# A hybrid encoder block on one core: the recurrence's preparations earlier among the input blocks, its chunks spread over six blocks, gate products inside the chunks

## The chip, the cores and the metric

The kernel runs on one core of a Trainium2 chip. The metric is the device time of one execution in microseconds (us); the median of three runs of the kernel before is 879.84 us (878.81 to 880.39). The engines are TensorE (PE: matmuls, with its weight loads as PEld), VectorE (DVE), ScalarE (ACT), GpSimd (POOL) and SyncE (SP, which issues most DMAs). Every engine works through its own instructions strictly in its own order.

## What is computed

One layer of a streaming encoder, for 512 positions of width 1024. The part that matters here is the first third: an input projection, a recurrence over 8 heads of 64 (branch a), a gated linear recurrence of width 512 behind a convolution over four positions (branch b), and their merge. Cross-attention and a convolutional feed-forward network (FFN) follow and are not touched.

```python
h = rms_norm(x, norm_mix_g[l])
proj = h @ w_in[l] + b_in[l]          # 38 blocks of 128 columns
y_a = rwkv7_branch(proj[..., :cb0], ...) @ w_branch_a[l]
y_b = rglru_branch(proj[..., cb0:cb1], proj[..., cb1:cb2], ...) @ w_branch_b[l]
merged = sigmoid(proj[..., cb2:cg1]) * y_a + sigmoid(proj[..., cg1:]) * y_b
x = x + merged @ w_mix_out[l]
...
# rwkv7_recurrence, per head and position
sa = state @ a_t
state = state * w_t + sa * b_t + v_t * k_t
y_t = state @ r_t
...
# rglru_branch
xb = causal_dwconv(px, conv_w, conv_b)
gate_a, gate_x = sigmoid(xb * w_ga + b_ga), sigmoid(xb * w_gx + b_gx)
h_t = a_t * h_(t-1) + xb_t * gate_x_t * mult_t
y = h * gelu(py)
```

## The kernel before

**Input blocks.** `inproj(i)` (L645) makes block i of the projection, the PSUM tile `in_ps{i}`, with 48 matmuls of 256 columns. A float32 weight is split in two fp32r halves, `win_h` (cast on ACT, L176) and `win_l` (the rest, on DVE, L177), and the product is made of three terms. The halves have three buffers each in the pool `wp` (L118), the raw weights four, so the casts of one block's weights can only begin when PE has finished the block three places earlier. Weights are streamed in the order IN_ORDER: blocks 12, 13, 4, 5, 0, 1, 8, 9, 6, 7, 2, 3, 10, 11 (those of the recurrence), then 22 to 37 (the merge's gates), 14 to 17 (branch b's convolution input) and 18 to 21 (its gelu gate). PSUM has three buffers for these tiles (`mm_ps`, L129), so a block starts only when the block three earlier has been read out.

**Preparations.** For each head pair j = 0 to 3, blocks 4+j (k), j (r) and 8+j (v) are read out with the shift over positions (`evac_shift`, L651). `prep(j)` (L673) makes the decay and rate (PE tiles psw, psa; a scan `L` and exponentials); `prep2(j)` (L691) normalizes k (PE tile ss) and writes the operands AK and KBt on DVE; `scores(j)` (L739) makes 32 small products within the 8 chunks of 64 positions (PE tiles sc), which are masked back into AK and BZ and sent to DRAM as dM; `bonus_terms(j)` (L716) makes the bonus, which is read back and multiplied later (`bonus`, L721, PE tiles bo). The loop over `jp` (L769) works on two pairs at a time, and NEARLY = 3 gate blocks (22 to 24) stand ahead of the last preparation.

**Inverse.** Once dM is complete, it is loaded as Nm, and 31 steps on DVE (L820 and L821: `zz`, `Zt`) invert the 32x32 diagonal blocks. The result goes to DRAM and comes back as ZA and as a part of BZ (L837, L842); PE completes the 64x64 inverses with zh0, zo0, zh16, zo16.

**Chunks.** `chunk(c)` (L911), for c = 0 to 7 in turn, is a chain through PE, ACT and DVE: x (PE), a copy Xs (DVE), u (PE), copies into UV (ACT and DVE), s (PE), Sn and the next UV (DVE), and x of the next chunk. vr and kbr put rows into chunk form, y is the output. PSUM has one buffer each for the tags kv, xu, y and s.

**Branch b.** `px_gates(b)` (L1002) reads block 14+b into xb with one ACT and three DVE instructions (L1007) and a fix (L1009), multiplies it by two gate weights (PE tiles ga, gx) and makes the gates; `px_scan(b)` (L1022) finishes the gates and scans into YB (L1029). xb has two buffers, so xb2 takes the place of xb0 when px_scan(0) is done, and xb3 that of xb1. ga, gx and the group norm's gv0, gg0 share one PSUM buffer. `group_norm` (L973) normalizes half of branch a's output.

**The order on PE** is written out by hand: `ORDER` (L40) lists PE's tiles, `name:n` for the next n matmuls of a tile, a bare name for all that are left of it, and `PE.arrange` (L100, called behind the last product) ties each matmul to the one before it. The small float32 products stand between input blocks, so that PE has in_ps matmuls to do while the other engines work on the chain. DVE's and ACT's order is that of the program with priorities; casts of weights have a high one.

**Sums.** NSUM (L642) says how many sums of FFN weights POOL issues behind which input block.

Of the kernel before, what the change touches and what calls it, by code (L numbers as in the profile page):

```python
# [41 lines left out]
ORDER = """  # L42
in_ps4 in_ps5 in_ps0 in_ps1 in_ps8 in_ps9 psw0 psa0 ss0 in_ps6 in_ps7 in_ps2:6 sc0 in_ps2:12 psw1 psa1 in_ps2:18
ss1 in_ps2 in_ps3 in_ps10:30 sc1 in_ps10 in_ps11 psw2 psa2 ss2 in_ps22 in_ps23 in_ps24:6 sc2 in_ps24 psw3 psa3
ss3 in_ps25 in_ps26 in_ps27:30 sc3 in_ps27 in_ps28 bo0 in_ps29 bo1 in_ps30 bo2 in_ps31 bo3 in_ps32 in_ps33
in_ps34 in_ps35 in_ps36 in_ps37 in_ps14 in_ps15:42 ga0 in_ps15 in_ps16:2 gx0 in_ps16:38 ga1 in_ps16:6 zh0 gx1
in_ps16 in_ps17:4 zo0 zh16 in_ps17:10 zo16 in_ps17:10 vr0 in_ps17:6 x0 y0:8 kbr0 in_ps17:2 u0 vr1 in_ps17:6 s0
y0 kbr1 in_ps17:4 x1 y1:8 in_ps17:2 u1 vr2 in_ps17 s1 y1 kbr2 in_ps18:8 x2 y2:8 in_ps18:4 u2 vr3 s2 y2 kbr3 ga2
in_ps18:2 x3 y3:8 gx2 u3 vr4 s3 y3 kbr4 ga3 x4 y4:8 u4 vr5 gx3 s4 y4 kbr5 in_ps18:6 x5 y5:8 u5 vr6 in_ps18:6 s5
y5 kbr6 in_ps18:2 x6 y6:8 vr7 in_ps18:2 u6 in_ps18:10 s6 y6 kbr7 in_ps18 gv0_0:1 in_ps19:8 x7 y7:8 in_ps19:6 u7  # L50
in_ps19:6 gv0_0 y7 in_ps19:4 gg0_0 in_ps19:20 gv0_1 in_ps19 in_ps20:16 gg0_1 in_ps20 in_ps21 gv1_0 gg1_0 gg1_1
yb_ps0:18 yb_ps1:10 gv1_1 yb_ps1:8 yb_ps0 yb_ps1 yb_ps2 yb_ps3 yb_ps4 yb_ps5 yb_ps6 yb_ps7 ya_ps0 ya_ps1 ya_ps2
ya_ps3 ya_ps4 ya_ps5 ya_ps6 ya_ps7 mix_ps0 mix_ps1 mix_ps2 mix_ps3 mix_ps4 mix_ps5 mix_ps6 mix_ps7 q_ps0_0:32
rxc_ps q_ps0_0 q_ps0_1 q_ps1_0:24 sc_ps0_0 sc_ps0_1 q_ps1_0 q_ps1_1:4 sc_ps0_2 prT_ps0:2 q_ps1_1:8 sc_ps0_3
prT_ps0:2 q_ps1_1:18 prT_ps0 q_ps1_1:10 o_ps0 q_ps1_1 o_ps1 q_ps2_0:4 sc_ps1_0 sc_ps1_1 q_ps2_0:16 sc_ps1_2
prT_ps1:2 sc_ps1_3 prT_ps1:2 q_ps2_0:16 prT_ps1 q_ps2_0:10 o_ps2 q_ps2_0 q_ps2_1:18 o_ps3 q_ps2_1 q_ps3_0:16
sc_ps2_0 sc_ps2_1 q_ps3_0:14 sc_ps2_2 prT_ps2:2 sc_ps2_3 prT_ps2:2 q_ps3_0:16 prT_ps2 q_ps3_0 q_ps3_1:16 o_ps4
q_ps3_1:16 o_ps5 q_ps3_1 co_ps0:16 sc_ps3_0 sc_ps3_1 co_ps0:14 sc_ps3_2 prT_ps3:2 sc_ps3_3 prT_ps3:2 co_ps0:6
co_ps4:10 prT_ps3 co_ps4:10 o_ps6 co_ps4:12 o_ps7 co_ps4:4 co_ps0:6 co_ps4:6 co_ps0 co_ps4 co_ps1
""".split()  # L60


# [17 lines left out]
def hybrid_block_kernel(ctx: ExitStack, tc: tile.TileContext, xT_d, mT_d, pv_d, cst_d, win_d, wk_d, wv_d,  # L80
                        lup_d, gup_d, rga_d, rgx_d, wba_d, wbb_d, wmix_d, wq_d, wo_d, wfi_d, wfo_d, out_d):
    nc = tc.nc
    V, S = nc.vector, nc.scalar
# [76 lines left out]
    def stream(dram, name, between=None, order=None, at=0):  # L160

        for g in order or range(dram.shape[0]):
            with tc.high_priority():
# [9 lines left out]
                wdma.append(ins)
                hi, lo = weight_tiles(name, g, at)
                for o in range(0, 1024, n):
                    casts.append(S.copy(hi[:, o:o + n], raw[:, o:o + n]))  # L176
                    V.tensor_tensor(lo[:, o:o + n], raw[:, o:o + n], hi[:, o:o + n].bitcast(F32), ALU.subtract)  # L177
# [466 lines left out]

    def inproj(i):  # L645
        nonlocal last_in
        ps = mm_ps(f"in_ps{i}")
        last_in = dense(ps, uin, lambda kb: (h2[:, 0, kb, :], h2[:, 1, kb, :]), KB, NSUM.get(i, 0))
        return ps

    def evac_shift(ps, blk, out):  # L651
# [3 lines left out]
        V.scalar_tensor_tensor(out, ps, omu[:, blk:blk + 1], q, ALU.mult, ALU.add)  # L655
# [107 lines left out]
    def gate_block(b):  # L763
        ps = inproj(22 + b)
        sg = tp.tile([P, T], F32, tag="st", name=f"gs{b}", bufs=2)
        tab(sg, ps, AF.Sigmoid, bias=par("b_in", 22 + b))
        nc.scalar.dma_start(dG[b], sg)

    for jp in range(2):  # L769
        js = (2 * jp, 2 * jp + 1)  # L770
        pks, prs = {}, {}
        for j in js:
            pks[j] = pp.tile([P, T], F32, tag="pk", name=f"pk{j}", bufs=2)
            evac_shift(inproj(4 + j), 4 + j, pks[j])
        for j in js:
            prs[j] = pp.tile([P, T], F32, tag="pr", name=f"pr{j}", bufs=3)
            evac_shift(inproj(j), j, prs[j])
        for j in js:
            evac_shift(inproj(8 + j), 8 + j, vT[:, j, :])
        for j in js:  # L780
            if j == 3:
                for i in IN_REST[:NEARLY]:
                    gate_block(i - 22)
            at, L, Pp = prep(j)
            prep2(j, pks[j], prs[j], at, L, Pp)
            scores(j)
            bonus_terms(j, pks[j], prs[j])
# [19 lines left out]
    with tc.tile_pool(name="pz", bufs=1, reuse_waits="tile") as pz:
        Nm = pz.tile([P, 32, 32], F32, name="Nm")
        Zt = pz.tile([P, 32, 32], F32, name="Zt")
        Zn = pz.tile([P, 32, 32], F32, name="Zn")  # L810
# [5 lines left out]
        V.memset(Zt.rearrange("p a b -> p (a b)")[:, 0:1024:33], 1.0)  # L816
        for s in range(30, -1, -1):
            n = 31 - s
            t3 = zz[:, 0:n * n].rearrange("p (a b) -> p a b", b=n)
            V.tensor_tensor(t3, Zt[:, s + 1:, s + 1:], Nm[:, s:s + 1, s + 1:].to_broadcast([P, n, n]), ALU.mult)  # L820
            V.tensor_reduce(Zt[:, s + 1:, s:s + 1], t3, AX.X, ALU.add)  # L821
# [804 lines left out]
```

## Time and profile before

| | |
|---|---|
| median of three runs | 879.84 us |
| profiled execution | 879.42 us, span 877.6 us |
| PE busy | 855.6 us, 97% |
| DVE busy | 679.5 us, 77% |
| ACT busy | 514.0 us, 59% |
| POOL busy | 132.5 us, 15% |
| granted TensorE clock | 0.998 |

A row of a timeline gives the start and the duration in us, the engine, the line, the operation, the tiles (out<-in), how many instructions, and in brackets the idle time before them with what ended it. A row of a window gives its length, and then for each engine its busy time and in (x...) its instructions; PEclk, the share of the DMA engines and GB/s stand at its end. A row of groups gives total busy us, mean ns of one, and the idle time before them.

### The profile page before, as it was taken

What the parts mean: (1) busy time and instruction counts of PE and PEld (TensorE: products, weight loads), DVE (VectorE), ACT (ScalarE), POOL (GpSimd) and SP (SyncE); (2) the same over time, 40 slices, a digit from 0 to 9 for tenths busy, and PEclk for the clock granted to TensorE, in tenths of its full rate; (3) what the DMA queues carried; (4) which work ended last, traced back from release to release, by engine and by line L of the source; (5) the groups of instructions that cost most, each with busy time, mean ns of one, the idle gap of its engine ahead of it and who ended that gap; (6) DMA issues with size and microseconds to landing.
All of it is one profiled execution on the core that took longest, in us unless ns stands there. A gap on an engine that the chain in (4) does not pass through costs nothing.

```text
span 877.6 us, 19313 instructions
## 1 busy us (share of the span) xinstructions
PE 855.6 (97%) x7884; PEld 825.9 (94%) x7884; DVE 679.5 (77%) x1096; ACT 514.0 (59%) x788; POOL 132.5 (15%) x163
## 2 busy tenths in 40 slices
PE   9999989999999999999999999999999999999996
PEld 8889989999997789999999899999999999999996
DVE  6796598877967686685575568799888888999774
ACT  7575676743437687234454356666666566867563
POOL 0102223021101022001122211102111121111100
PEclk9999999999999999999999999999999999999999
DMA  8888799777895479858987858999999999998953
...
DMA packets 97576, 201.60 MB, mean 230 GB/s; under 512 B 19600, under 2 KB 30992, under 8 KB 97424
## 3 DMA queue, kind: packets, MB, share of 16 engines
...
q8 instruction: 62, 1.02, 0.5%
...
## 4 chain that ended last, share of the span: by engine, by line
PE 74%; DVE 13%; ACT 5%; DMA 4%; issue 3%; DVEq 0%; ACTq 0%; SPq 0%
PE fx_ps L95 14%; PE in_ps L95 13%; PE fyz_ps L95 10%; PE ox_ps L95 7%; PE oyz_ps L95 5%; PE co_ps L95 5%; PE mix_ps L95 4%; PE q_ps L95 4%; PE yb_ps L95 2%; DVE win_l L177 2%; PE v_ps L95 2%; PE o_ps L95 1%; PE k_ps L95 1%; DVE Zt L821 1%; DVE zz L820 1%
## 5 line engine op out<-in xcount | busy, mean ns | idle before, releaser
L95 PE MATMUL in_ps<-hT,win_h 128*128 128x256 f32 x1216 | 214.8, 280 | 2.1 <-DVE pr L655 1.6
L95 PEld LDWEIGHTS in_ps<-hT,win_h 128*128 128x128 f32 x1216 | 185.1, 188 | 6.1 <-DVE pr L655 1.8
L95 PE MATMUL in_ps<-hT,win_l 128*128 128x256 f32 x608 | 170.2, 280 | 1.1 <-DVE win_l L177 1.1
L199 ACT CAST wfi_h<-wfi_r 128x1024 fp32r<-128x1024 f32 x77 | 80.9, 1051 | 69.7 <-PE fyz_ps L95 25.2
L95 PEld LDWEIGHTS in_ps<-hT,win_l 128*128 128x128 f32 x608 | 114.2, 188 | 3.2 <-DVE win_l L177 1.7
L551 POOL DMA_DIRECT2D dS<-in_wfi x66 | 66.8, 1032 | 304.3 <-PE in_ps L95 127.5
L200 DVE TENSOR_TENSOR wfi_l<-wfi_r,wfi_h 128x1024 fp32r<-128x1024 f32 x77 | 94.1, 1222 | 19.8 <-ACT wfi_h L199 19.8
L177 DVE TENSOR_TENSOR win_l<-win_r,win_h 128x1024 fp32r<-128x1024 f32 x38 | 46.3, 1221 | 25.5 <-ACT win_h L176 25.2
L587 POOL DMA_DIRECT2D dOs<-in_wfo x54 | 39.9, 820 | 168.0 <-PE fx_ps L95 45.8
L95 PE MATMUL fx_ps<-hq,wfi_h 128*128 128x256 f32 x352 | 61.2, 276 | 0.0
L95 PE MATMUL fx_ps<-hr,wfi_h 128*128 128x256 f32 x352 | 61.1, 276 | 0.0
L95 PE MATMUL fyz_ps<-hq,wfi_h 128*128 128x256 f32 x352 | 61.1, 276 | 0.0
L95 PE MATMUL ox_ps<-go,wfo_h 128*128 128x256 f32 x352 | 59.9, 276 | 0.0
L176 ACT CAST win_h<-win_r 128x1024 fp32r<-128x1024 f32 x38 | 39.7, 1045 | 34.1 <-PE in_ps L95 31.1
L1436 DVE TENSOR_TENSOR wfo_l<-wfo_r,wfo_h 128x1024 fp32r<-128x1024 f32 (+1 forms) x39 | 47.2, 1213 | 11.6 <-ACT wfo_h L1435 11.6
L1435 ACT CAST wfo_h<-wfo_r 128x1024 fp32r<-128x1024 f32 (+1 forms) x39 | 40.4, 1036 | 25.1 <-DMA wfo_r<-dOs 8.2
L95 PEld LDWEIGHTS fx_ps<-hr,wfi_h 128*128 128x128 f32 x352 | 53.1, 188 | 0.2 <-ACT sn L1371 0.2
L95 PEld LDWEIGHTS fx_ps<-hq,wfi_h 128*128 128x128 f32 x352 | 53.2, 188 | 0.0
L95 PEld LDWEIGHTS fyz_ps<-hq,wfi_h 128*128 128x128 f32 x352 | 53.1, 188 | 0.0
L95 PEld LDWEIGHTS ox_ps<-go,wfo_h 128*128 128x128 f32 x352 | 52.9, 188 | 0.0
L95 PE MATMUL fyz_ps<-hq,wfi_l 128*128 128x256 f32 x176 | 48.7, 277 | 0.6 <-DVE wfi_l L200 0.6
L95 PE MATMUL fx_ps<-hq,wfi_l 128*128 128x256 f32 x176 | 48.6, 276 | 0.0
...
## 6 DMA issues: line engine op xcount, KB each, us to landing
...
```

The lines of the kernel that those rows point to most:

```text
L95: return self.log(out, nc.tensor.matmul(out, *args, **kw))
L176: casts.append(S.copy(hi[:, o:o + n], raw[:, o:o + n]))
L177: V.tensor_tensor(lo[:, o:o + n], raw[:, o:o + n], hi[:, o:o + n].bitcast(F32), ALU.subtract)
L199: S.copy(hi, raw)
L200: V.tensor_tensor(lo, raw, hi.bitcast(F32), ALU.subtract)
L551: return lambda: nc.gpsimd.dma_start(s(out), src, **kw)
L587: yield lambda k=k, w=w, src=src: nc.gpsimd.dma_start(dO[n, m][:, k * P:(k + w) * P], src, **kw)
L820: V.tensor_tensor(t3, Zt[:, s + 1:, s + 1:], Nm[:, s:s + 1, s + 1:].to_broadcast([P, n, n]), ALU.mult)
L821: V.tensor_reduce(Zt[:, s + 1:, s:s + 1], t3, AX.X, ALU.add)
L1435: S.copy(hi[:, :n], raw[:, :n])
L1436: V.tensor_tensor(lo[:, :n], raw[:, :n], hi[:, :n].bitcast(F32), ALU.subtract)
```

## The change

It does six things. All computation stays the same; only the order of emission and the order on the engines change.

1. The loop over pairs becomes a list of steps, RWKV_STEPS (i: a block, p: prep, k: prep2, f: scores and bonus terms). Preparation j starts as soon as its blocks allow.
2. In ORDER psw, psa, ss and sc of each pair move forward: sc0 from in_ps2 to behind in_ps8, sc1 from in_ps10 into in_ps2, sc2 from in_ps24 into in_ps11, sc3 from in_ps27 into in_ps24. Between psw3 and sc3 there stand in_ps23 and 24 matmuls of in_ps24; before, in_ps25, in_ps26 and 30 matmuls of in_ps27.
3. zh0 moves from in_ps16 into in_ps14. The chunks then run through in_ps15 to in_ps21 with 12 matmuls of a block at three or four places of each chunk; before, they had in_ps17 to in_ps19, in unequal pieces, with in_ps20 and in_ps21 whole behind them.
4. ga and gx stand in chunks 0 to 4 (before: ga0, gx0, ga1, gx1 ahead of the chunks), gv0 and gg0 in chunks 6 and 7; gv1_0 and gg1 move behind the first yb_ps.
5. ZCASTS holds the inverse's step n on DVE behind the low cast of weight group g.
6. NEARLY becomes 2, and NSUM moves sums within in_ps16 to in_ps21.

```diff
-NEARLY = 3
+NEARLY = 2
+RWKV_STEPS = """i4 i5 p0 i0 k0 i1 i8 f0 i9 p1 k1 i6 i7 f1 i2 p2 k2 i3 i10 f2 i11 i22 p3 k3 i23 f3""".split()
+ZCASTS = ((5, 20), (12, 21), (17, 22), (21, 23), (24, 24), (26, 25), (28, 26), (30, 27))
...
-ss3 in_ps25 in_ps26 in_ps27:30 sc3 in_ps27 in_ps28 bo0 in_ps29 bo1 in_ps30 bo2 in_ps31 bo3 in_ps32 in_ps33
-y0 kbr1 in_ps17:4 x1 y1:8 in_ps17:2 u1 vr2 in_ps17 s1 y1 kbr2 in_ps18:8 x2 y2:8 in_ps18:4 u2 vr3 s2 y2 kbr3 ga2
+psw2 psa2 ss2 in_ps3 in_ps10 in_ps11:36 sc2 in_ps11 in_ps22 psw3 psa3 ss3 in_ps23 in_ps24:24 sc3 in_ps24 in_ps25
+in_ps16:12 s0 y0 kbr1 gx0 in_ps16:12 x1 y1:8 in_ps16:12 u1 vr2 ga1 in_ps17:12 s1 y1 kbr2 gx1 in_ps17:12 x2 y2:8
+in_ps17:12 u2 vr3 in_ps17:12 s2 y2 kbr3 ga2 in_ps18:12 x3 y3:8 gx2 in_ps18:12 u3 vr4 in_ps18:12 s3 y3 kbr4
...
-            37: 1, 17: 4, 18: 5, 19: 5, 20: 2, 21: 1}
+            37: 1, 16: 3, 17: 3, 18: 3, 19: 3, 20: 3, 21: 2}
...
-    for jp in range(2):
-        js = (2 * jp, 2 * jp + 1)
...
+    for step in RWKV_STEPS:
+        what, n = step[0], int(step[1:])
+        if what == "i":
+            rwkv_block(n) if n < 12 else gate_block(n - 22)
+        elif what == "p":
+            Ls[n] = prep(n)
+        elif what == "k":
+            prep2(n, pks[n], prs[n], *Ls[n])
+        else:
+            finish(n)
...
-        if k > 2:
-            bonus(k - 3, bhi[:, k - 3, :], blo[k - 3], last_in)
+        j = k + NEARLY - 6
+        if j >= 0:
+            bonus(j, bhi[:, j, :], blo[j], last_in)
...
-            if i == 19:
+            if i == 21:
                 for jp in range(2):
                     group_norm(0, jp, rw_ps(f"gv0_{jp}", prg, "rg"), rw_ps(f"gg0_{jp}", prg, "rg"))
...
     PE.arrange(ORDER)
+    for n, g in ZCASTS:
+        tc.add_manual_dep(steps[n].ins, lows["win", g].ins.name, mybir.DependencyInfo(
+            mybir.DependencyClass.NoSync, mybir.DependencyReason.DATA), reason="order of the casts")
```

Line numbers are higher in the kernel after, by 2 to 14 (L655 becomes L659, L1007 becomes L1021).

Two places in detail. First DVE in the last preparation, from the scan of L3 to the last write of KBt, which sc3 waits for. Before:

```order
L683 SCALAR_TENSOR_TENSOR L3_2077<-cst_76,L3_2077 128x512
L688 COPY PC_761<-Pp3_2082 128x8
L714 TENSOR_TENSOR AK_760<-pr3_1628,Pp3_2082 64x8x64 x2
L177 TENSOR_TENSOR win_l20_2356<-win_r20_2353,win_h20_2355 128x1024
L700 SCALAR_TENSOR_TENSOR kk3_2088<-sq3_2090,kk3_2088 128x512
L704 SCALAR_TENSOR_TENSOR AK_760<-kk3_2088,Pp3_2082 64x8x64 x2
L705 TENSOR_TENSOR kk3_2088<-kk3_2088,at3_2079 128x512
L710 TENSOR_TENSOR KBt_758<-kk3_2088,L3_2077 64x8x64 x2
L707 TENSOR_TENSOR pk3_1504<-pk3_1504,at3_2079 128x512
L711 TENSOR_TENSOR KBt_758<-pk3_1504,L3_2077 64x8x64
L177 TENSOR_TENSOR win_l21_2422<-win_r21_2419,win_h21_2421 128x1024
L711 TENSOR_TENSOR KBt_758<-pk3_1504,L3_2077 64x8x64
```

After:

```order
L687 SCALAR_TENSOR_TENSOR L3_1960<-cst_76,L3_1960 128x512
L692 COPY PC_761<-Pp3_1965 128x8
L718 TENSOR_TENSOR AK_760<-pr3_1671,Pp3_1965 64x8x64 x2
L180 TENSOR_TENSOR win_l18_2239<-win_r18_2236,win_h18_2238 128x1024
L704 SCALAR_TENSOR_TENSOR kk3_1971<-sq3_1973,kk3_1971 128x512
L708 SCALAR_TENSOR_TENSOR AK_760<-kk3_1971,Pp3_1965 64x8x64 x2
L709 TENSOR_TENSOR kk3_1971<-kk3_1971,at3_1962 128x512
L714 TENSOR_TENSOR KBt_758<-kk3_1971,L3_1960 64x8x64 x2
L711 TENSOR_TENSOR pk3_1466<-pk3_1466,at3_1962 128x512
L715 TENSOR_TENSOR KBt_758<-pk3_1466,L3_1960 64x8x64 x2
```

The sequence is the same, with one cast of weights in it in place of two. On PE the distance between psw3 and sc3 has shrunk as point 2 says.

Second DVE in chunk 2, ahead of ga2, which needs xb2 complete. Before, xb2 (from in_ps16) is written in chunk 0, where its last write is the row of xb2 and dp:

```order
L1007 SCALAR_TENSOR_TENSOR xb2_4023<-in_ps16_3968,pv_75,xb2_4023 128x511
L1028 TENSOR_TENSOR xb1_3937<-xb1_3937,gx1_3948 128x512
L933 COPY UV0_2865<-u0_1_2907 64x256
L1029 SCALAR_TENSOR_TENSOR YB_2615<-ga1_3947,xb1_3937 128x512
L1007 SCALAR_TENSOR_TENSOR xb2_4023<-in_ps16_3968,pv_75,xb2_4023 128x510
L1007 SCALAR_TENSOR_TENSOR xb2_4023<-in_ps16_3968,pv_75,xb2_4023 128x509
L949 TENSOR_TENSOR Sn0_2954<-s0_2930,PC_761 128x256
L1009 TENSOR_TENSOR xb2_4023<-xb2_4023,dp_686 128x3
```

After, chunk 2's copy of u into UV2 comes first, four rows of px_scan(0) follow (gx0, xb0, YB), and then these rows up to xb2's last write:

```order
L963 TENSOR_TENSOR Sn2_3106<-s2_3082,PC_761 128x256
L180 TENSOR_TENSOR win_l36_4259<-win_r36_4256,win_h36_4258 128x1024
L967 TENSOR_TENSOR UV3_3070<-Sn2_3106,SP1_3034 64x256 x2
L974 TENSOR_TENSOR SP2_3110<-UV3_3070,PC_761 64x256 x2
L1040 SCALAR_TENSOR_TENSOR gx1_3948<-ga1_3947,gx1_3948 128x512
L1021 SCALAR_TENSOR_TENSOR xb2_4026<-in_ps16_3968,pv_75,xb2_4026 128x511
L1041 MEMSET gx1_3948 128x1
L1021 SCALAR_TENSOR_TENSOR xb2_4026<-in_ps16_3968,pv_75,xb2_4026 128x510
L1042 TENSOR_TENSOR xb1_3937<-xb1_3937,gx1_3948 128x512
L1021 SCALAR_TENSOR_TENSOR xb2_4026<-in_ps16_3968,pv_75,xb2_4026 128x509
L1043 SCALAR_TENSOR_TENSOR YB_2615<-ga1_3947,xb1_3937 128x512
L1023 TENSOR_TENSOR xb2_4026<-xb2_4026,dp_686 128x3
```

xb2 has moved two chunks back. On PE, ga2 stands at the same place in chunk 2 as before, but with less between it and its predecessors on DVE; what PE has there now, from the end of the piece behind vr3 to the next block:

```order
L97 MATMUL in_ps17_4043<-hT2_1_88,win_h33_4046 128x256
L97 MATMUL in_ps17_4043<-hT2_0_87,win_l33_4047 128x256
L97 MATMUL s2_3082<-UV2_2994,KBr2_3023 64x64 x8
L97 MATMUL y2_3049<-BZ_757,UV2_2994 64x64 x8
L100 MATMUL kbr3_3100<-cst_76,KBt_758 128x128 x4
L97 MATMUL ga2_4032<-xb2_4026,rg_765 128x512
L97 MATMUL in_ps18_4132<-hT2_0_87,win_h34_4135 128x256
L97 MATMUL in_ps18_4132<-hT2_1_88,win_h34_4135 128x256
```

ga2 comes right behind kbr3, as before; gx1 stands at the end of chunk 1, before it stood ahead of all chunks.

More of the change, by code (lines that the diff above doesn't have):

```diff
@@ L51 @@
[L51 to L59, printed above, removed]
+in_ps4 in_ps5 psw0 psa0 in_ps0 ss0 in_ps1 in_ps8 sc0 in_ps9 psw1 psa1 ss1 in_ps6 in_ps7 in_ps2:12 sc1 in_ps2
@@ new lines @@
+psw2 psa2 ss2 in_ps3 in_ps10 in_ps11:36 sc2 in_ps11 in_ps22 psw3 psa3 ss3 in_ps23 in_ps24:24 sc3 in_ps24 in_ps25
+in_ps26 in_ps27 in_ps28 bo0 in_ps29 bo1 in_ps30 bo2 in_ps31 bo3 in_ps32 in_ps33 in_ps34 in_ps35 in_ps36 in_ps37
+in_ps14:24 zh0 in_ps14 zo0 zh16 in_ps15:18 zo16 in_ps15:18 vr0 in_ps15 x0 y0:8 kbr0 in_ps16:12 u0 vr1 ga0
+in_ps16:12 s0 y0 kbr1 gx0 in_ps16:12 x1 y1:8 in_ps16:12 u1 vr2 ga1 in_ps17:12 s1 y1 kbr2 gx1 in_ps17:12 x2 y2:8
+in_ps17:12 u2 vr3 in_ps17:12 s2 y2 kbr3 ga2 in_ps18:12 x3 y3:8 gx2 in_ps18:12 u3 vr4 in_ps18:12 s3 y3 kbr4
@@ new lines @@
+in_ps18:12 x4 y4:8 ga3 in_ps19:12 u4 vr5 gx3 in_ps19:12 s4 y4 kbr5 in_ps19:12 x5 y5:8 in_ps19:12 u5 vr6
+in_ps20:12 s5 y5 kbr6 in_ps20:12 x6 y6:8 in_ps20:12 u6 vr7 in_ps20:12 s6 y6 kbr7 gv0_0 in_ps21:12 x7 y7:8 gg0_0
+in_ps21:12 u7 gv0_1 in_ps21:12 y7 gg0_1 in_ps21:12 yb_ps0:18 yb_ps1:18 gv1_0 gg1_0 yb_ps0 yb_ps1 yb_ps2:6 gv1_1
+gg1_1 yb_ps2 yb_ps3 yb_ps4 yb_ps5 yb_ps6 yb_ps7 ya_ps0 ya_ps1 ya_ps2 ya_ps3 ya_ps4 ya_ps5 ya_ps6 ya_ps7 mix_ps0
+mix_ps1 mix_ps2 mix_ps3 mix_ps4 mix_ps5 mix_ps6 mix_ps7 q_ps0_0:32 rxc_ps q_ps0_0 q_ps0_1 q_ps1_0:24 sc_ps0_0
@@ L60 @@
+o_ps7 co_ps4:4 co_ps0:6 co_ps4:6 co_ps0 co_ps4 co_ps1
 """.split()
@@ L152, in hybrid_block_kernel @@
     wdma, mdma, casts = [], [], []
+    lows = {}
     OFF = 32
@@ L767, in gate_block, with rwkv_block, finish @@
         nc.scalar.dma_start(dG[b], sg)
-    for jp in range(2):
-        js = (2 * jp, 2 * jp + 1)
[L771 to L787, printed above, removed]
+    pks, prs, Ls = {}, {}, {}
+    def rwkv_block(i):
+        j = i % 4
+        if i < 4:
+            out = prs[j] = pp.tile([P, T], F32, tag="pr", name=f"pr{j}", bufs=3)
+        elif i < 8:
+            out = pks[j] = pp.tile([P, T], F32, tag="pk", name=f"pk{j}", bufs=2)
+        else:
+            out = vT[:, j, :]
+        evac_shift(inproj(i), i, out)
+    def finish(j):
+        scores(j)
+        bonus_terms(j, pks[j], prs[j])
+    for step in RWKV_STEPS:
[6 more added lines that the diff above has]
+            prep2(n, pks[n], prs[n], *Ls[n])
+        else:
+            finish(n)
     pp_ctx.close()
@@ L816, in hybrid_block_kernel @@
         V.memset(Zt.rearrange("p a b -> p (a b)")[:, 0:1024:33], 1.0)
+        steps = []
         for s in range(30, -1, -1):
```

17 lines of the change are left out of this document (9 added, 8 removed).

## The prediction

> **What bounds the kernel now.** I read the page first, then the list of waits, then TensorE's (PE's) timeline with start times. The page's first block:
>
> ```profile
> span 877.6 us, 19313 instructions
> PE 855.6 (97%) x7884; PEld 825.9 (94%) x7884; DVE 679.5 (77%) x1096; ACT 514.0 (59%) x788; POOL 132.5 (15%) x163
> ```
>
> PE is busy for 97% of the span, so an edit that leaves its matmuls alone can win only what PE loses between them. The profiled execution took 879.42 us around its span of 877.6; the median of the runs is 879.84, that is 0.42 more, and I add that at the end. The longest wait of PE where the change works (total, times, longest):
>
> ```profile
> PE in_ps L95 <- DVE pr L655: 1.6, 1, 1.6
> ```
>
> All others are smaller, and idle time understates them: a stall also costs the matmuls' start anew. So I price pieces from start to start. Three matmuls of an input block, in PE's timeline:
>
> ```profile
> 250.78 0.39 PE L95 MATMUL in_ps<-hT,win_h 128*128 128x256 f32 x2
> 251.01 0.28 PE L95 MATMUL in_ps<-hT,win_l 128*128 128x256 f32 x1
> 251.12 0.39 PE L95 MATMUL in_ps<-hT,win_h 128*128 128x256 f32 x2
> ```
>
> They take 251.12 - 250.78 = 0.34 us, 0.113 each; an input block of 48 takes 5.44.
>
> **Preparations (65 to 187 us).** The last matmuls of each preparation, sc0 to sc3, stall a little before the change. The first and the last of the four, as windows from the first sc matmul to the next tile:
>
> ```profile
> 113.35:116.36 3.01, 2.44 (x34) 2.15 (x33) 2.67 (x5) 2.57 (x4) 0.00 (x0) 1.00 1.07 369
> 181.96:184.98 3.02, 2.43 (x33) 2.15 (x33) 2.61 (x5) 0.00 (x0) 0.00 (x0) 1.00 0.80 247
> ```
>
> I estimate 1.9 us for one without a stall, so the four lose about 1.1 each, 4.4. With the 1.6 of the list and about 0.9 of small ones (psw1, ss2) the stage waits for 6.9 us.
>
> Now the last preparation. On PE, psw3 starts it; on VectorE (DVE) it ends with the second write of KBt, and sc3 needs that:
>
> ```profile
> 166.20 0.39 PE L95 MATMUL psw<-pwa,lhi 128*128 128x512 f32 x1
> ```
> ```profile
> 168.65 1.23 DVE L683 TENSOR_TENSOR_SCAN L<-cst,L 128x512 f32<-128x512 f32 x1
> 171.18 0.17 DVE L688 COPY PC<-Pp 128x8 f32<-128x8 f32 x1 [1.30 <-ACT Pp L322]
> 174.19 1.23 DVE L177 TENSOR_TENSOR win_l<-win_r,win_h 128x1024 fp32r<-128x1024 f32 x1 [1.56 <-ACT win_h L176]
> 180.96 1.21 DVE L177 TENSOR_TENSOR win_l<-win_r,win_h 128x1024 fp32r<-128x1024 f32 x1
> 182.20 0.69 DVE L711 TENSOR_TENSOR KBt<-pk,L 64x512 f32<-64x512 f32 x1
> ```
>
> That is 182.89 - 166.20 = 16.7 us. Before, two whole blocks and 30 matmuls lay between psw3 and sc3, 14.3 us with psa3 and ss3. After, it is one block and 24 matmuls: 5.44 + 2.72 + 1.37 (six matmuls of 512 columns, 166.20 to the next block at 167.57) = 9.5. DVE's order keeps the whole chain and loses one cast (the row at 180.96), so the chain is 16.7 - 1.2 = 15.5, and **sc3 waits 15.5 - 9.5 = 6.0 us**. Without the two waits for ScalarE (ACT), 1.30 and 1.56, the chain would be 12.6 and the wait 3.1; if one more cast of ACT falls into it, 7. The other preparations have more cover. Walking DVE's and ACT's orders in the same way I get 1.3 for ss0 (two blocks after in4 now), 0.5 for sc0, 0.7 for sc1, 1.2 for ss2 (behind sc1's evacuations) and none for sc2: 3.7, with bounds 0 and 6. The stage then waits for 9.7 instead of 6.9: **+2.8**.
>
> **The casts before in_ps14 (227 to 251 us).** The inverse is a chain of 62 DVE instructions, and the weight casts that stand behind it come late:
>
> ```profile
> 227.11:251.12 24.01, 22.89 (x194) 22.19 (x193) 0.00 (x0) 2.73 (x4) 1.00 0.86 253
> 203.16 0.16 DVE L820 TENSOR_TENSOR zz<-Zt,Nm 128x1 f32<-128x1 f32 x1 [4.23 <-DMA Nm<-dM]
> 243.40 1.16 DVE L821 TENSOR_REDUCE Zt<-zz 128x31 f32<-128x961 f32 x1
> ```
>
> Four blocks take 24.0 instead of 4 x 5.44 = 21.8: 2.2 lost. The eight tuples place each low cast (1.2 us) ahead of an inverse step, and my walk finds each in time by 0.3 to 0.5 us. I take a loss of 0.2: **-2.0** (bounds -2.2 and +1, if the casts miss). The inverse itself starts 20.3 us after the last KBt (182.89 to 203.16), through DRAM, and its result goes through DRAM again:
>
> ```profile
> 254.68 1.16 SPq L837 DMA_DIRECT2D ZA<-dZt  x2
> ...
> DMA to landing us min/median/max: 3.6/3.8/4.0
> ```
> ```profile
> 264.88 1.20 PE L95 MATMUL zh<-ZA,BZ 32*32 32x32 f32 x64
> ```
>
> The second ZA is issued near 255.3 and lands by 259.3, 5.6 us ahead of zh0. After, by my walk from psw3 (near 153), KBt ends near 168.7, 14.2 earlier; two casts more among its steps leave ZA some 12.5 us earlier, near 246.7. zh0 stands behind half of in14 instead of behind in16: before, that place was at 251.12 - 2.72 = 248.4, and with +2.8 and -2.0 it is 249.2. So ZA is still 2.5 us ahead, and the DMA chain stays covered; its price if it isn't is a rival below.
>
> **Chunks and gates (251 to 344 us).** Steady prices, start to start, from one chunk and one gate product of before:
>
> ```profile
> 278.72 0.68 PE L95 MATMUL u<-Xs,BZ 64*64 64x64 f32 x16
> 279.56 0.68 PE L95 MATMUL vr<-cst,vT 64*64 64x64 f32 x16 [0.15 <-ACT KBr L905]
> 280.17 0.39 PE L95 MATMUL in_ps<-hT,win_l 128*128 128x256 f32 x1
> ...
> 281.06 0.69 PE L95 MATMUL s<-UV,KBr 128*64 128x64 f32 x16
> 281.68 0.68 PE L95 MATMUL y<-BZ,UV 64*64 64x64 f32 x16
> 282.29 0.66 PE L98 MATMUL kbr<-cst,KBt 128*128 128x128 f32 x4
> 282.70 0.37 PE L95 MATMUL in_ps<-hT,win_l 128*128 128x256 f32 x1
> ...
> 294.55 1.02 PE L95 MATMUL ga<-xb,rg 128*128 128x512 f32 x2
> 295.74 0.69 PE L95 MATMUL x<-UV,AK 128*64 128x64 f32 x16
> 296.26 0.64 PE L95 MATMUL y<-AK,UV 128*64 128x64 f32 x16
> ```
> ```profile
> 344.38 0.47 PE L95 MATMUL yb_ps<-yb,wbb_h 128*128 128x256 f32 x1
> ```
>
> From in15's first matmul (251.12) to yb_ps0's (344.38) PE needs 93.3 us. By these prices the stretch holds 336 x 0.113 = 38.1 of in_ps, 8 x 0.51 of ga and gx, 4 x 1.2 of zh and zo, 8 x 0.61 of vr, 8 x 0.52 of x, 16 x 0.61 of y, 8 x 0.41 of kbr, 7 x 0.62 of s, 8 x about 0.5 of u, and about 3.6 of gv and gg: 81.1. So 12.2 are lost. PE's busy share shows only 2.0 of that as idle:
>
> ```profile
> 274.00:344.00 70.00, 68.00 (x1032) 59.01 (x1031) 52.26 (x99) 49.81 (x88) 11.68 (x13) 1.00 0.65 159
> ```
>
> Where in_ps matmuls are put between the small float32 tiles, each piece costs about 0.2 extra (six took 0.89 from 280.17 to s at 281.06, for 0.68). Before has 31 such pieces: 6.2. The remaining 6.0 are waits of the chunk's chain. After, pieces of 12 matmuls (1.56 us with the extra) stand evenly at three or four places of each chunk: 28 pieces, -0.6, and a copy of 0.4 between x and u or u and s is covered. I leave 0.5 for the last chunk: **-5.5** (bounds -2.0, what shows as idle, and -6.0).
>
> **The new wait at ga2.** ga and gx of all four conv blocks now stand inside chunks 0 to 4. xb has two buffers, so xb2 can only be written when xb0's scan is done, and DVE works strictly in order. After, between the copy of chunk 2's u (UV2) and the last write of xb2 stand 16 rows of its order. Their prices, groups of DVE between 255 and 300 us:
>
> ```profile
> L177 DVE TENSOR_TENSOR win_l<-win_r,win_h 128x1024 fp32r<-128x1024 f32 x3 | 3.7, 1227 | 3.3 <-ACT win_h L176 3.3
> L1007 DVE SCALAR_TENSOR_TENSOR xb<-in_ps,pv,xb 128x509 f32<-128x509 f32 x4 | 3.0, 746 | 0.1
> L960 DVE TENSOR_TENSOR SP<-UV,PC 64x256 f32<-64x256 f32 x6 | 2.5, 420 | 0.2
> L1029 DVE TENSOR_TENSOR_SCAN YB<-ga,xb 128x512 f32<-128x512 f32 x2 | 2.5, 1226 | 0.1
> L1026 DVE SCALAR_TENSOR_TENSOR gx<-ga,gx 128x512 f32<-128x512 f32 x2 | 1.4, 692 | 0.4 <-ACT gx L322 0.3
> ```
>
> Copy of u 0.42, as one of SP; two L1026 and two products of the same size 4 x 0.69; two scans 2 x 1.23; Sn and the pairs of UV and SP 5 x 0.42; a cast 1.23; three L1007 3 x 0.75; three tiny ones 0.3. Sum: 0.42 + 2.76 + 2.46 + 2.10 + 1.23 + 2.25 + 0.3 = 11.5 us from the end of u2. On PE, u2 and ga2 are now only vr3 0.61, twelve in_ps 1.56, s2 0.62, y2 0.61 and kbr3 0.41 apart: 3.8. So **ga2 waits about 7.7 us**, with s3, u3 and all else queued behind it on PE, since PE keeps its order. Bounds: 7.0, if the small steps overlap, to 9, if gx0 or gx1 comes late from ACT. Before, gx1 came right behind zh0 (264.88), thirty microseconds ahead of ga2 (294.55), which had no wait. What follows finds DVE ahead again, so nothing is paid twice; and nothing that PE loses here is given back, as PE is the bound afterwards.
>
> The last products gv1 and gg1 among the yb_ps keep their small wait: +0.2. NSUM moves sums that GpSimd issues (POOL, busy for 15%); there are 17 behind in_ps16 to in_ps21 before and after, and no stage here reads them: nothing.
>
> Sum without the next step: 2.8 - 2.0 - 0.6 - 5.5 + 7.7 + 0.2 = +2.6, so 879.42 + 2.6 = 882.0, 882.4 against the median.
>
> **TensorE's speed after a long wait.** No wait of PE in this trace is longer than 1.6 us, and none slows it. But at the start of the program the array is slow, although the granted clock reads 1.00 there. Compare the first 17 matmuls of 512 columns with later ones of that size:
>
> ```profile
> 1.07 5.77 PE L95 MATMUL wake<-onesr 128*128 128x512 f32 x17 [1.07 <-DVE Pp L685]
> ```
> ```profile
> 29.71 0.62 PE L95 MATMUL v_ps<-wv_h,m 128*128 128x512 f32 x2
> 30.17 0.39 PE L95 MATMUL v_ps<-wv_l,m 128*128 128x512 f32 x1
> ```
>
> Later two take 0.46, 0.23 each. The first 16 starts spread over 5.77 - 0.39 = 5.4 us, 1.7 more than 16 x 0.23. A wait of 6.0 or 7.7 us lies nearer to that than to the 1.6 that costs nothing: it is longer than the whole slow stretch. I take one such restart for each of the two waits, 2 x 1.7 = **3.4**, bounds 0 and 3.4. The Trainium skill, TensorE: Matmul & The Clock Gate, section What's actually happening, says that the array falls to half rate after an idle window of about 3.4 us and needs about as long a busy one to return. The wake rows agree with its second half; no run here shows the first. By that rule the result is 885.8, and without it 882.4.
>
> **Rivals.**
> 1. *Both waits, no restart*: the 1.6 us wait costs no speed, and perhaps 8 doesn't. 882.4, chance 0.22; the restart decides 3.4 us.
> 2. *The preparations have no late DVE* (faster): if ACT's waits of 1.30 and 1.56 leave the last chain and the four lesser waits don't come, sc3 waits 3.1 and the array isn't slowed there. 885.8 - 2.9 - 3.7 - 1.7 = 877.5. For it: 2.9 us of the chain are idle time of DVE. Against it: the chain's order is unchanged, and its two waits came from casts and exponentials that are still there. It decides from where KBt's last write comes within 12.6 us of psw3. Chance 0.13.
> 3. *The chunks gain more*: even pieces also save the 0.2 each. -5.6 of the 28 pieces: 880.2, or 876.8 if there is no restart. Chance 0.08.
> 4. *The inverse comes late*: the path from sc3 through DRAM to ZA grows by over 2.3 us, and PE waits at zh0; with casts that miss their steps some 3 us more: 889. For it: the steps and casts now alternate exactly. Against: no partial sums of the weights are issued between blocks 24 and 26, where sc3's transfers now fall. Chance 0.07.
> 5. *The waits that go and come cancel*: about 879.8, chance 0.05.
>
> **How the numbers follow.** The forecast has both new waits and both restarts: 882.0 + 3.4 = 885.4, 885.8 against the median; chance 0.45. The range runs from 876 (below it only part of cases 2 and 3) to 889.5 (case 4 beyond). A measurement of this kernel tells 0.2%, 1.8 us, from no change. Faster: case 2, half of case 3 and a little of case 5's spread, 0.20. Same: the other half of 3, case 5 and the lowest part of case 1 (below 881.6), 0.14. Slower: the rest, 0.66.
>
> **What would show it.** In the profile after: a wait of PE at sc for DVE's KBt of 4 to 7 us, one at ga for DVE's xb of 7 to 9, in35 to in14 at 5.44 a block, zh0 without a wait, no chunk wait over 0.6 us, and in_ps or small tiles at about half rate for some 3 us behind the two long waits. I am wrong if either long wait is under 3 us, if zh waits, or if the matmuls behind both waits keep 0.113 us.

## The result and the profile after

The kernel after takes 892.25 us (median of four runs, 892.22 to 892.42), the kernel before on the same chip 880.06: ratio 1.0144 (95% interval 1.0132 to 1.0156), 12.2 us slower. The prediction was 885.8 with a range to 889.5. The direction was right; half of the loss was missing.

The page of the kernel after (busy time, and PE and its granted clock in 40 slices of 22 us):

```profile
span 890.6 us, 19306 instructions
PE 858.9 (96%) x7884; PEld 830.4 (93%) x7884; DVE 679.0 (76%) x1096; ACT 514.3 (58%) x788; POOL 132.8 (15%) x163
...
PE   9999999799999699999999999999999999999996
...
PEclk9999999999999799999999999999999999999999
```

The matmuls are the same, but PE is busy for 3.3 us longer: for a while it was slower. The two new dips of PE (7 and 6 tenths) are at 156 to 178 and 289 to 312 us, and the clock dips with the second. The longest waits of PE (total, times, longest):

```profile
PE ga L97 <- DVE xb L1023: 8.1, 1, 8.1
PE sc L97 <- DVE KBt L715: 5.2, 1, 5.2
PE zh L97 <- DMA ZA<-dZt: 1.9, 1, 1.9
PE gg L97 <- ACT y L326: 1.3, 1, 1.3
```

The first two were forecast at 7.7 and 6.0. The third was a rival; the fourth belongs to the last chunk, for which the prediction left 0.5 in all. What each stage lost shows in windows cut at the same work in both kernels: from in_ps4 to in_ps28, to in_ps14, to yb_ps0, to mix_ps0. First before, then after:

```profile
67.67:187.14 119.47, 115.27 (x1018) 111.52 (x1017) 92.25 (x153) 75.79 (x107) 21.26 (x23) 1.00 0.84 215
187.14:245.44 58.30, 57.19 (x490) 56.29 (x489) 48.25 (x85) 21.34 (x28) 10.48 (x11) 1.00 0.83 231
245.44:344.38 98.94, 96.52 (x1464) 84.61 (x1463) 69.03 (x122) 65.13 (x109) 13.06 (x14) 1.00 0.70 170
344.38:389.32 44.94, 44.55 (x388) 44.16 (x387) 33.88 (x49) 16.60 (x22) 3.00 (x3) 1.00 0.78 221
```
```profile
67.96:190.28 122.32, 116.02 (x1018) 112.69 (x1017) 101.91 (x189) 77.93 (x111) 23.17 (x25) 0.99 0.84 215
190.28:246.58 56.30, 56.30 (x491) 55.99 (x489) 39.96 (x50) 19.27 (x24) 8.63 (x9) 1.00 0.92 242
246.58:355.24 108.66, 96.64 (x1455) 85.54 (x1453) 64.98 (x116) 61.67 (x103) 16.07 (x17) 0.94 0.68 164
355.24:402.27 47.03, 46.65 (x398) 45.97 (x397) 36.03 (x52) 20.18 (x27) 0.00 (x0) 1.00 0.56 173
```

The first numbers are the lengths: +2.85, -2.0, +9.7 and +2.1. Three small products (gv1_0, gg1_0, gg1_1: 1.8 us by their rows after) moved from the third stage to the fourth; with them put back it is +11.5 and +0.3. So the third stage, from in_ps14 through the chunks, holds nearly all of the loss. PE's timeline there, at zh0:

```profile
251.40 1.26 PE L97 MATMUL zh<-ZA,BZ 32*32 32x32 f32 x64 [1.94 <-DMA ZA<-dZt]
252.59 0.80 PE L97 MATMUL in_ps<-hT,win_h 128*128 128x256 f32 x2
253.18 0.41 PE L97 MATMUL in_ps<-hT,win_l 128*128 128x256 f32 x1
253.39 0.63 PE L97 MATMUL in_ps<-hT,win_h 128*128 128x256 f32 x2
```

and at ga2:

```profile
302.80 2.04 PE L97 MATMUL ga<-xb,rg 128*128 128x512 f32 x2 [8.10 <-DVE xb L1023]
303.86 1.42 PE L97 MATMUL in_ps<-hT,win_h 128*128 128x256 f32 x2
305.07 0.41 PE L97 MATMUL in_ps<-hT,win_l 128*128 128x256 f32 x1
...
307.22 0.69 PE L97 MATMUL x<-UV,AK 128*64 128x64 f32 x16
```

Behind both waits a pair of in_ps matmuls lasts 0.63 us and more and a single one 0.41, where 0.39 and 0.28 are normal: the array runs at about half speed. The twelve behind ga2 take 3.36 us (303.86 to 307.22) and ga2 itself 1.06; at full speed the twelve behind gx2 take 1.89 (308.87 to 310.76) and gx2 0.56. So the slow rows at ga2 cost 2.0 us beside the wait.

The granted clock shows where slow rows begin and end. Windows of the kernel after, with the clock as the last number but two:

```profile
160.24:163.66 3.42, 1.66 (x15) 1.46 (x13) 3.34 (x5) 2.42 (x3) 0.00 (x0) 1.00 1.09 306
167.07:170.49 3.42, 3.40 (x26) 3.13 (x28) 2.33 (x4) 1.14 (x2) 0.00 (x0) 0.50 0.65 250
248.99:252.40 3.41, 1.47 (x67) 1.27 (x67) 0.00 (x0) 0.00 (x0) 0.00 (x0) 1.00 0.98 285
252.40:255.82 3.42, 3.42 (x29) 3.36 (x22) 0.70 (x1) 0.58 (x1) 0.00 (x0) 0.50 1.01 405
296.78:307.02 10.24, 4.22 (x14) 3.21 (x14) 8.07 (x15) 2.79 (x4) 0.70 (x1) 0.50 0.17 52
```

The clock is halved for 3.41 us at sc3 (167.07) and at zh0 (252.40), and for three times that around ga2 (296.78). The three beginnings lie 85.33 and 44.38 us apart, which is 25 and 13 times 3.413: in this trace the clock changes only in steps of 3.41 us, and not at the moment at which a wait begins or ends. A step with 1.47 us of work in it (248.99 to 252.40) was followed by half speed; one with 1.66 (160.24 to 163.66) was not, and at sc3 the clock fell only behind the next step, in which TensorE stood still throughout.

ga2 waits for what the prediction named. DVE's timeline, from the copy of u2 to xb2's last write (the rows left out follow back to back):

```profile
291.06 0.43 DVE L947 COPY UV<-u 64x256 f32<-64x256 f32 x1 [2.30 <-PE u L97]
291.96 0.69 DVE L1040 SCALAR_TENSOR_TENSOR gx<-ga,gx 128x512 f32<-128x512 f32 x1 [0.47 <-ACT gx L326]
...
301.39 1.22 DVE L1043 TENSOR_TENSOR_SCAN YB<-ga,xb 128x512 f32<-128x512 f32 x1
302.52 0.14 DVE L1023 TENSOR_TENSOR xb<-xb,dp 128x3 f32<-128x3 f32 x1
```

302.66 - 291.06 = 11.6, forecast 11.5.

zh0 waits for the way through DRAM. The inverse ended 19 us earlier than before (the first DMA of its result, dZt, is issued at 225.3, before at 244.6), but what follows took longer. SyncE's queue, and the landing of ZA:

```profile
225.31 0.47 SPq L838 DMA_DIRECT2D dZt<-Zt  x1
226.49 1.34 SPq L840 DMA_DIRECT2D dZ<-Zn  x2
...
234.77 4.93 SPq L856 DMA_DIRECT2D BZ<-dZ  x3
239.76 3.43 SPq L851 DMA_DIRECT2D ZA<-dZt  x2
...
DMA to landing us min/median/max: 6.1/8.5/11.0
```

dZ is back after 8 us (226.5 to 234.8; before 246.8 to 252.3), issuing the reads takes 8.4 us, where it took 3.6 before, and the two reads of ZA land in 6.1 and 11.0 us, before in 3.6 and 4.0. The later one, issued at 240.4, ends zh0's wait at 251.4. From dZt's issue to zh0's start it is 26 us; before, ZA had landed 15 us after it.

### The profile page after: what moved, and what is told of

The parts are those of the page before. It is cut to its first block, busy times and chain, and to the rows that moved or that the text cites. A ratio compares the mean times of both kernels' runs of the same rounds, so it can differ in the third digit from the quotient of the medians.

```text
span 890.6 us, 19306 instructions
## 1 busy us (share of the span) xinstructions
PE 858.9 (96%) x7884; PEld 830.4 (93%) x7884; DVE 679.0 (76%) x1096; ACT 514.3 (58%) x788; POOL 132.8 (15%) x163
## 4 chain that ended last, share of the span: by engine, by line
PE 76%; DVE 13%; DMA 4%; ACT 3%; issue 2%; SPq 1%; DVEq 0%; ACTq 0%
PE fx_ps L97 13%; PE in_ps L97 12%; PE fyz_ps L97 10%; PE ox_ps L97 7%; PE oyz_ps L97 5%; PE co_ps L97 5%; PE mix_ps L97 4%; PE q_ps L97 4%; PE yb_ps L97 2%; DVE zz L833 2%; PE v_ps L97 2%; DVE win_l L180 2%; PE o_ps L97 1%; DVE Zt L835 1%; PE k_ps L97 1%
## 5 line engine op out<-in xcount | busy, mean ns | idle before, releaser
L97 PE MATMUL in_ps<-hT,win_h 128*128 128x256 f32 x1216 | 219.4, 284 | 0.5 <-DVE hT L457 0.5
L97 PEld LDWEIGHTS in_ps<-hT,win_h 128*128 128x128 f32 x1216 | 187.6, 190 | 7.5 <-issue 4.4
```

Source lines behind the costliest of these rows:

```text
L97: return self.log(out, nc.tensor.matmul(out, *args, **kw))
```

## The experiments

Each is the kernel after with an edit; the change is against its 892.25 us. Three or five rounds beside the kernel before on the same chip. Beside them the kernel before took 879.57 to 880.54 us (medians), so a difference under about 1 us is not told apart.

**ga2 later.**

> The kernel after, with ga2, gx2, ga3 and gx3 each moved 9 to 10 us later in TensorE's order (ga2 behind kbr4). Theory (xb2 is late because VectorE's queue is full, and only ga2's place makes TensorE wait for it): in VectorE's order Xs3 now stands ahead of px_scan(1) and of xb2, so u3 has its input in time; ga2 waits under 1 us, and 8.1 + 0.2 + 2.6 = 10.9 us go, to 881.3 to 882.5. Rival (VectorE has more work in chunks 2 to 4 than TensorE, so the wait only moves to u3, s3 or ga2's new place): 886 to 892.

```diff
-in_ps17:12 u2 vr3 in_ps17:12 s2 y2 kbr3 ga2 in_ps18:12 x3 y3:8 gx2 in_ps18:12 u3 vr4 in_ps18:12 s3 y3 kbr4
-in_ps18:12 x4 y4:8 ga3 in_ps19:12 u4 vr5 gx3 in_ps19:12
+in_ps17:12 u2 vr3 in_ps17:12 s2 y2 kbr3 in_ps18:12 x3 y3:8 in_ps18:12 u3 vr4 in_ps18:12 s3 y3 kbr4 ga2
+in_ps18:12 x4 y4:8 gx2 in_ps19:12 u4 vr5 ga3 in_ps19:12 gx3
```

883.12 us, ratio to the kernel before 1.0042 (1.0027 to 1.0057): 9.1 us gone. ga2 starts without a wait; what is left of DVE's queue is a wait of x3:

```profile
PE x L96 <- DVE UV L966: 0.6, 1, 0.6
```

Most of the cost was ga2's place. The theory had 10.9 us; what remains are small waits such as that at x3.

**The array kept busy in the wait.** Three kernels put 36, 27 and 18 matmuls on constants ahead of ga2.

```diff
+        if b == 2:
+            for k in range(36):
+                PE.matmul(psa, onesr, onesr.unsqueeze(1).to_broadcast([P, 4, P]), start=True, stop=True)
         PE.matmul(psa, rg[:, 0, b, :], xb, start=True, stop=True)
```

> The kernel after, with 36 matmuls of 512 columns on constants (0.227 us each, 8.2 us) put on TensorE between kbr3 and ga2, written to ga2's own PSUM buffer and overwritten by it. The wait for xb2 stays, but the array is busy in it. Theory (the wait costs a second time, since the array runs slowly behind it): the granted clock at 300 to 310 us returns to 1.00, ga2 takes 0.5 instead of 1.05 and the twelve in_ps18 behind it 1.6 instead of 3.4, so the time falls by 2.3 to 2.6 us, to about 889.8. Rival (the slow rows behind ga2 have another cause, such as the restart of one stalled instruction): 892.3, no change.

888.81 us, ratio 1.0103 (1.0088 to 1.0118): 3.4 us less. The window of 300 to 310 us, first of the kernel after, then of this one (the clock is the last number but two):

```profile
300.00:310.00 10.00, 7.20 (x55) 5.51 (x56) 5.40 (x10) 2.00 (x3) 0.70 (x1) 0.65 0.20 52
```
```profile
300.00:310.00 10.00, 10.00 (x137) 8.17 (x137) 4.55 (x10) 3.87 (x7) 1.86 (x2) 1.00 0.32 64
```

The clock is back at 1.00. From ga2's start to x3's it is 2.40 us here (300.51 to 302.91), in the kernel after 4.42 (302.80 to 307.22): the slow rows behind ga2 come from the standstill, and cost 2.0 us. The rest is mostly zh0, which the edit does not touch: in the profiled run it waited 0.9 from ZA, and no slow rows followed.

> As the kernel with 36 matmuls ahead of ga2, but with 18: TensorE works for 4.1 us of the wait and then stands still for about 4.2. Theory (the array falls back to half speed after an idle time of 2 to 4 us, however long it worked before): ga2 and the twelve in_ps18 are slow again, granted clock at 300 to 310 us well under 1, 892 to 892.5. Rival (it takes over 4.2 us of idle time): the rows behind ga2 at full speed, 889.5.

> As the kernel with 36 matmuls ahead of ga2, but with 27: TensorE works for 6.1 us of the wait and then stands still for about 2.0. With 18 (4.0 us of idle time) the rows behind ga2 were slow, with 36 (0.1) they weren't. Theory (an idle time of 3 to 4 us is what slows the array): ga2 and in_ps18 at full speed, 889 to 890. Rival (2 us are enough, as at zh0, where 1.9 us were followed by slow rows): slow again, 892 to 893.

893.76 us with 18 (ratio 1.0150, 1.0128 to 1.0172) and 891.38 with 27 (1.0121, 1.0104 to 1.0139). Behind 4.0 us of standstill the rows are slow; behind 1.9 us the twelve in_ps18 are just as slow (3.5 us, 302.66 to 306.13), so the theory of 3 to 4 us fell, though the time with 27 lies between its two forecasts. With 27, at ga2, and the window in which the clock is halved:

```profile
302.13 1.51 PE L97 MATMUL ga<-xb,rg 128*128 128x512 f32 x2 [1.92 <-DVE xb L1023]
302.66 1.40 PE L97 MATMUL in_ps<-hT,win_h 128*128 128x256 f32 x2
303.87 0.41 PE L97 MATMUL in_ps<-hT,win_l 128*128 128x256 f32 x1
...
306.13 0.69 PE L97 MATMUL x<-UV,AK 128*64 128x64 f32 x16
```
```profile
302.68:306.09 3.41, 3.41 (x14) 2.71 (x12) 2.25 (x3) 0.75 (x2) 0.70 (x1) 0.50 0.00 0
```

ga2 itself still ran at full speed (0.53 from its start to the next); the clock fell at the end of the step in which the wait lay. Whether a wait of 2 us costs more than itself thus depends also on how it lies among the steps, and no trace of the kernel before shows that.

In the kernel before, the wait of 1.6 us ahead of in_ps10 was followed by rows at full speed:

```profile
130.95:133.67 2.72, 2.72 (x23) 2.72 (x24) 2.72 (x4) 1.74 (x3) 1.51 (x2) 1.00 0.64 200
```

**The sums away from the inverse's DMAs.**

> The kernel after, with the five sums of FFN weights behind in_ps33 to in_ps37 moved behind in_ps16 to in_ps20. Theory (ZA comes late because the transfers of dZ and ZA meet the sums' 512 KB transfers): ZA lands in about 4 us as in the kernel before instead of 8.5, dZ in 5.5 instead of 8.8, zh0 doesn't wait, and 1.9 + 1.7 = 3.6 us go, to about 888.6. Rival (the loads of win_r make the traffic, which run ahead now that casts are in time): zh0 still waits over 1 us, 891 to 892.5.

```diff
-            22: 2, 23: 1, 27: 1, 28: 1, 29: 1, 31: 1, 32: 1, 33: 1, 34: 1, 35: 1, 36: 1,
-            37: 1, 16: 3, 17: 3, 18: 3, 19: 3, 20: 3, 21: 2}
+            22: 2, 23: 1, 27: 1, 28: 1, 29: 1, 31: 1, 32: 1,
+            16: 4, 17: 4, 18: 4, 19: 4, 20: 4, 21: 2}
```

889.62 us, ratio 1.0114 (1.0099 to 1.0129): 2.6 us less. zh0 doesn't wait:

```profile
225.19 0.47 SPq L838 DMA_DIRECT2D dZt<-Zt  x1
226.37 1.10 SPq L840 DMA_DIRECT2D dZ<-Zn  x2
...
230.43 3.63 SPq L856 DMA_DIRECT2D BZ<-dZ  x3
234.12 1.68 SPq L851 DMA_DIRECT2D ZA<-dZt  x2
...
DMA to landing us min/median/max: 4.2/4.4/4.5
```

The inverse ends at the same time, and ZA is issued 5.6 us earlier and lands 4 us faster. What made the way long is the sums' transfers. From in_ps14's start to in_ps15's it is 8.97 us (246.91 to 255.88), in the kernel after 12.49 (246.58 to 259.07): zh0 cost 3.5. About 1 us of the 3.6 expected did not come, and 0.8 of it is at sc3, where nothing was edited: from in_ps24 to in_ps25 it is 15.75 us in this profiled run (158.55 to 174.30) and 14.95 in that of the kernel after (159.02 to 173.97). The wait is 5.2 in both, but here the clock is halved for two steps:

```profile
165.01:171.84 6.83, 5.21 (x35) 4.72 (x36) 5.62 (x10) 1.87 (x4) 0.00 (x0) 0.50 0.56 217
```

**sc3 later, alone and without the sums.**

> The kernel after, with sc3 behind in_ps25's first half instead of in_ps24's. Theory (the wait at sc3 is on the path that ends at ZA, and zh0 stands too early for ZA): sc3 waits under 1 us, but the inverse starts only some 1 to 2 us earlier (the slow sc3 of 4.0 us becomes 2), so zh0 waits 5 to 7 us instead of 1.9 and the time falls by only 1 to 3 us, to 889 to 891. Rival (the two waits are independent): 5.2 + 2.2 = 7.4 go, to 885.

```diff
-ss3 in_ps23 in_ps24:24 sc3 in_ps24 in_ps25
+ss3 in_ps23 in_ps24 in_ps25:24 sc3 in_ps25
```

886.88 us (885.59 to 889.63), ratio 1.0076 (1.0059 to 1.0093): 5.4 less, between theory and rival, and its runs differ by 4 us. In the profiled one, the slowest, the wait at sc3 is nearly gone and that at zh0 has grown:

```profile
PE zh L96 <- DMA ZA<-dZt: 3.4, 1, 3.4
...
PE sc L96 <- DVE KBt L714: 1.1, 2, 0.7
```

> The kernel after with sc3 later and the five sums out of the way, ga2 as in the kernel after. Theory (with ZA landing in time, the wait at sc3 and its slow rows are gained in full): zh0 doesn't wait, and 7.4 of sc3 (less 2 that it still loses) and 2.6 of the sums go, 883 to 885. Rival (zh0 comes too early for ZA in spite of it): over 886.

883.88 us, ratio 1.0043 (1.0028 to 1.0057), as expected: 8.4 less than the kernel after and 5.7 less than without the sums alone. By the medians sc3's place is thus worth 5.4 us with the sums in the way and 5.7 without them: the two waits are nearly independent, as the rival had it, though with less than its 7.4. The exchange that the theory expected, sc3's wait coming back at zh0, shows in the slowest run alone.

**Group norm later.**

> The kernel after, with gg0_0, gv0_1 and gg0_1 each one piece of twelve in_ps21 (or 18 yb_ps) later on TensorE. Theory (they stand closer behind each other than ScalarE's and VectorE's steps between them allow, in one shared PSUM buffer): the 1.3 us ahead of gg0_0 and the 0.7 ahead of gv0_1 go and nothing new over 0.5 comes, so the time is 890.2 to 890.8. Rival (the normalization is late at the end of branch a anyway, and the wait moves to gg0_1, gv1_0 or yb_ps): 891.5 to 892.5.

```diff
-gv0_0 in_ps21:12 x7 y7:8 gg0_0 in_ps21:12 u7 gv0_1 in_ps21:12 y7 gg0_1 in_ps21:12 yb_ps0:18 yb_ps1:18
+gv0_0 in_ps21:12 x7 y7:8 in_ps21:12 u7 gg0_0 in_ps21:12 y7 in_ps21:12 gv0_1 yb_ps0:18 gg0_1 yb_ps1:18
```

896.24 us, ratio 1.0187 (1.0170 to 1.0204): 4.0 slower. The 1.3 ahead of gg0_0 is gone, but gv1_1 is now late:

```profile
361.84 0.49 PE L96 MATMUL gv<-gv_h,bonesr 128*128 128x512 f32 x1 [0.86 <-ACT gv_h L230]
364.12 0.70 PE L96 MATMUL gv<-gv_l,bonesr 128*128 128x512 f32 x1 [1.79 <-DVE gv_l L231]
```

The rival was right, and by more than it said: the normalization is a chain that ends among the yb_ps, and a wait early in it is cheaper than one at its end. Slow rows come on top: the granted clock is 0.50 from 364.25 to 367.66.

**No ZCASTS.**

> The kernel after without ZCASTS: on VectorE the low casts of weight groups 22 to 27 fall one or two inverse steps later, other rows are the same. Theory (the casts' places are what brings in_ps32 to in_ps37 to 5.44 us a block): these blocks lose 1 to 2.5 us, the wait at zh0 shrinks by as much, since ZA lands as before, and the time is 891.5 to 893. Rival (the blocks are in time without it, since the whole inverse is 19 us earlier): no block over 5.5 us, 892.2.

```diff
-ZCASTS = ((5, 20), (12, 21), (17, 22), (21, 23), (24, 24), (26, 25), (28, 26), (30, 27))
+ZCASTS = ()
```

893.37 us, ratio 1.0147 (1.0130 to 1.0164), the same as with it (1.0144). Six blocks from in_ps32 to in_ps37 in this kernel:

```profile
215.46:248.11 32.65, 32.65 (x288) 32.65 (x288) 0.00 (x0) 4.09 (x6) 1.00 0.99 249
```

32.65 / 6 = 5.44 us a block, no loss. The theory fell: the casts are in time without ZCASTS. The inverse now ends near the start of in_ps34 (225.31 and 224.82 in the kernel after), which is the likely reason; no run shows that by itself.

**Edits together.**

> The kernel after with four edits together: ga2 to gx3 later, sc3 later, the five sums out of the way, and gg0 and gv0_1 later. Theory (the four waits are all that makes the kernel after slower, and the rest of the change, the casts in time and the even pieces, is a gain): the single gains of the four (9.1, 2.6, 7.4 where ZA is in time, 2.0) add up to 21, so 871 to 873, 7 to 9 below the kernel before. Rival (with sc3 no longer waiting, zh0 comes 5 to 6 us earlier than ZA allows, whatever the sums do): zh0 waits 3 to 5 us and slows the array, 876 to 880.

> The kernel after with three of the edits: ga2 to gx3 later, sc3 later, the five sums out of the way; gg0 and gv0_1 stand as in the kernel after. Theory (these three waits are the loss, and moving gg0 and gv0_1 only shifted waits behind yb_ps, for 2 to 4 us more): 3 us less than with all four edits, 873 to 876, and the chain of zh0, chunks and yb_ps has no wait over 1.4 us. Rival (the group norm's waits grow when the chunks end earlier): 877 to 879.

> The kernel with three edits, without ZCASTS as well. Theory (the casts are in time because the inverse starts earlier and not because of ZCASTS): the same time within 0.7 us, no block from in_ps32 to in_ps37 over 5.5 us. Rival (here in_ps32 to in_ps37 come 5.6 us earlier, and the casts behind the last inverse steps are late): 1 to 3 us slower.

All four edits: 877.81 us, ratio 0.9968 (0.9958 to 0.9978). That lies in the rival's range, but zh0 does not wait; the loss is at the group norm, with 1.8 us of wait at gv1_1 as in the kernel with that edit alone. Three edits: 874.58, ratio 0.9935 (0.9921 to 0.9949), 17.7 less than the kernel after and faster than the kernel before by 5.3 us. Three edits without ZCASTS: 874.71, ratio 0.9940 (0.9926 to 0.9954), the same. The single gains, 9.1 for ga2 and 8.4 for sc3 with the sums, add up to 17.5. Even here, in the profiled run (877.66, the slowest of five), one standstill of 0.7 us in zh16 was followed by slow rows: the next eighteen in_ps15 took 3.85 us (251.54 to 255.39) instead of 2.29.

## Why the prediction was right and wrong

The terms against the stages above (us). The measured parts come from the profiled runs, and the last row but two is what they leave of the stages:

| term | forecast | measured |
|---|---|---|
| preparations: waits, and slow rows behind sc3 | +2.8 +1.7 | +2.9 |
| casts ahead of in_ps14 | -2.0 | -2.0 |
| zh0: wait 2.0 and slow rows 1.5 | 0 | +3.5 |
| ga2: wait | +7.7 | +8.3 |
| ga2: slow rows | +1.7 | +2.0 |
| waits of gg0_0 and gv0_1 in chunk 7 | +0.5 | +1.8 |
| other waits and pieces of in_ps | -6.6 | -4.1 |
| from yb_ps0 on | +0.2 | +0.3 |
| sum | +6.0 | +12.7 |

- *The wait at ga2* was right in place, cause and size, and so were its slow rows in kind: the kernels with and without matmuls in the wait show them apart. They were under-sized by 0.3.
- *The wait at sc3* was 5.2, forecast 6.0, with 2.1 for its slow rows (the 32 products take 3.99 us, where the prediction estimated 1.9), forecast 1.7. The stage was still over-sized by 1.6, and the reason lies in the kernel before. By the prediction's own prices (18 blocks of 5.44, four sc of 1.9, four times six matmuls for 1.37) the stage needs 111.0 us. The kernel after loses 11.3 of its 122.3, as forecast (9.7 and 1.7); the kernel before lost 8.5 of its 119.5, where the prediction counted 6.9.
- *The step that failed* is "ZA is still 2.5 us ahead, and the DMA chain stays covered". The estimate of where the inverse ends was too late by 7 us, and that should have made it safer; but the duration of the way through DRAM was carried over from before, 3.8 us for a landing. In the kernel before it fell beside in_ps14 and in_ps15, behind which no sum is issued; after, it falls behind in_ps33 to in_ps37 with one each. The prediction looked at the sums near sc3's transfers and not at those near ZA's. ZA came 2.0 us late instead of 2.5 early, and with the slow rows zh0 cost 3.5 us that the sum had at nothing. The rival had the place and the mechanism with a chance of 0.07; "if zh waits" was one of the prediction's own signs of being wrong.
- *A second step*: "I leave 0.5 for the last chunk". gg0_0 stands 3.2 us behind gv0_0 in the new order; its wait of 1.3 shows that ACT and DVE need 4.5. With 0.5 at gv0_1 that is 1.3 more than was left. Moving them later did not win it back (896.24).
- *A cause that was wrong with a right number*: the casts are in time, -2.0, but not through ZCASTS. That is luck.
- *Pieces*: those behind a gate product cost about 0.5 extra rather than 0.2 (the piece from gx2 to u3: 1.89 instead of 1.56). Eight of them make 2.4 (an estimate, 8 times 0.3), about the 2.5 that the row of other waits and pieces lacks; no run tried it.

The rule of the Trainium skill, TensorE: Matmul & The Clock Gate, section What's actually happening, named the right kind of cost: half rate behind an idle window, until a busy one of about 3.4 us. The trace agrees with the length: 0.50 from 252.40 to 255.82. As for the condition, an idle window of about 3.4 us, 1.94 us of standstill within such a stretch were enough here, and the measurement decides.
